# Memory tiles asked for on GpSimd's queue, and cumulated decays read back by pairs of heads, in a hybrid decoder layer

## The chip, the core and the metric

The kernel runs on one core of a Trainium2 chip. The core has five engines that work through instruction queues of their own: TensorE (PE in the profile) multiplies matrices, VectorE (DVE) and ScalarE (ACT) do elementwise work, GpSimd (POOL) does some elementwise work and issues DMAs, and SyncE (SP) only issues DMAs. ScalarE issues some DMAs too. Every queue is worked off in order: an instruction that waits holds up all that stand behind it. The metric is the device time of one execution in microseconds (us), less is better.

## What is computed

The reference is one layer: a SwiGLU feed-forward block, a mixer with two head groups (a Mamba-2 scan, here SSD, and differential attention), cross-attention into a memory of 256 tokens, and a second SwiGLU block. There are 512 tokens of width 1024, all in float32. Two pieces of it are touched here. The first is the decay matrix of the SSD scan, for each of 16 heads and 4 chunks of 128 tokens:

```python
la_cum = jnp.cumsum(la, axis=2)
seg = la_cum[:, :, :, None] - la_cum[:, :, None, :]
decay = jnp.exp(jnp.where(causal[None, None, :, :, None, None], seg, -jnp.inf))
y_diag = jnp.einsum('bclsg,bclsgr,bcsgrp->bclgrp', cb, decay, xdt)
```

The second is the normed memory, which cross-attention projects into keys and values:

```python
k = (mem_n @ w_ck).reshape(bsz, mlen, CROSS_HEADS, CROSS_HEAD_DIM)
v = (mem_n @ w_cv).reshape(bsz, mlen, CROSS_HEADS, CROSS_HEAD_DIM)
```

## The kernel before

Activations lie transposed, with features on the 128 partitions and tokens along the free dimension. Every float32 matrix product is done as three products of a reduced type: `split_into` (L152) makes from a tile a high part on ScalarE (`wh`, `hm`, `ysh`; L155, or L159 where a scale is applied) and the rest on VectorE (`wl`, `hm` low, `ysl`; L156, L160), and `mm3` multiplies high by high, high by low and low by high. One weight tile of 128x1024 therefore costs a load on SP's queue (`load_w`, L172, issue on L174), one split on ScalarE, one on VectorE and then 24 matmuls of 512 columns (`proj`). The raw weights have six buffers and the split ones three, so a load waits for the split of the load six before it.

The program is made in Python by a small planner, `Order` (L57). It steps through dense generators (the projections, in a fixed list) and adds the time of each matmul to a clock; chains (norms, heads, the SSD groups) are spawned with a due time and step in between when the clock has passed it. What the generators issue on SP's and on GpSimd's queues stays in the order of issue. The order on ScalarE and VectorE is chosen by the framework's scheduler from the same program.

Around the change:

- `steps` (L606) computes the cumulated decays `cum` as 128 tokens x 4 chunks x 16 heads. It transposes the 64 columns on TensorE (`pct`), copies them to SBUF (`ct_sb`) and stores them in DRAM as `cum_d`, 64 rows of 128, with row number 16 x chunk + head.
- `decays(g, j)` (L829) reads them back for two heads of group `g`, broadcast over the partitions, into one of two buffers (`gate` for j = 0, `th` for j = 1). It is called once for group 0 at the end of `steps` and then inside `group`, after the products that used the buffer.
- `group(g, ...)` (L838) is the chain of one SSD group of four heads. For each pair of heads ScalarE takes the exponential of the rows (L899), eight Relu of 128x128 (L901) and two exponentials (L902), VectorE masks with `cbm` (L903), and TensorE then does `pf` and `py`.
- `group_dense(g)` (L813) is the dense work of a group: four projections `xbc_tile` (products `pxbc`, then a convolution, L805 and L808, and a silu, L796 and L797) and two projections `pz`.
- `memory_prep` (L966) asks for the eight memory tiles (128x256 each) and then splits one at each step of its chain. It runs twice: in the first feed-forward block for the keys, and from `group_dense(3)` for the values, whose products `pcv` stand behind the last attention output.
- `block_sums_in_dram` (L1148) is a chain that makes sums of weight blocks for the second feed-forward block, off the way: SP loads a block into DRAM tiles `isum` and `wsum` (L1161), and some steps later GpSimd adds another to it with an accumulating DMA (L1165).

Besides its data, a DMA waits for its completion counter. SP's and ScalarE's DMAs together take eight counters in turn, GpSimd's take eight of their own, and a DMA that takes a counter waits until the DMA that had it before has landed. In the program before, the last four of the second eight memory loads on SP take the counters of the four decay reads that ScalarE issued for group 2, so each waits for one of those to land.

Of the kernel before, what the change touches and what calls it, by code (L numbers as in the profile page):

```python
# [17 lines left out]
P = 128  # L18
T = 512
D = 1024  # L20
KT = D // P
# [27 lines left out]
C_FFN1, C_MIX, C_CROSS, C_MEM, C_FFN2, C_SSD = (8 * i for i in range(6))  # L49
# [51 lines left out]
def body(tc, a, dbg=None):  # L101
    nc = tc.nc
# [12 lines left out]
    def nm(s):  # L115
        uid[0] += 1
        return f"{s}_{uid[0]}"

    def s2(s, dt=F32, shape=(P, T)):
        if math.prod(shape[1:]) <= T // 2:  # L120
            return sp.tile(list(shape), dt, tag="s1", name=nm(s), bufs=NHALF)
        return sp.tile(list(shape), dt, tag="s2", name=nm(s))

    def s4(s):
        return sp.tile([P, 4, T // 2], F32, tag=s, name=nm(s), bufs=1)

    def small(s, n, bufs=None):
        return tiny.tile([P, n], F32, tag=s, name=nm(s), bufs=bufs)

    def acc(s, shape=(P, T)):  # L130
        return acc_p.tile(list(shape), F32, tag="acc", name=nm(s))

    def aux(s, shape=(P, T)):
        return aux_p.tile(list(shape), F32, tag="aux", name=nm(s))

    def dump(name, t):
        if dbg and name in dbg:
            nc.sync.dma_start(dbg[name], t.bitcast(F32) if t.dtype == R32 else t)

    last, start, last_sum, recent, newest, newest_mm = [], [], [], [], [], []  # L140
    V, S, G = nc.vector, nc.scalar, nc.gpsimd
    od = Order()

    def mm(out, w, x, start, stop):
        od.t += (1 if w.dtype == R32 else 4) * (x.free_size() + 8) / 2400
        newest_mm[:] = [nc.tensor.matmul(out, w, x, start=start, stop=stop).ins]  # L146

    def transpose(out, x):
        od.t += 2 * (P + 8) / 2400
        nc.tensor.transpose(out, x, ident)  # L150

    def split_into(hi, lo, src, scale=None):  # L152
        if scale is None:
            return (
                S.activation(hi, src, AF.Copy),  # L155
                V.tensor_tensor(lo, src, hi.bitcast(F32), ALU.subtract),  # L156
            )
        return (
            S.activation(hi, src, AF.Copy, scale=scale),  # L159
            V.scalar_tensor_tensor(lo, src, scale, hi.bitcast(F32), ALU.mult, ALU.subtract),  # L160
        )

    def split(s, src, scale=None, half=False, n=T):
        if half:
            both = s2(s, R32, (P, 2, T // 2))
            hi, lo = both[:, 0], both[:, 1]
        else:
            hi, lo = s2(s + "h", R32, (P, n)), s2(s + "l", R32, (P, n))
        last[:] = [i.ins for i in split_into(hi, lo, src, scale)]
        return hi, lo  # L170
# [12 lines left out]
    @contextmanager  # L183
    def behind(ins):
        with ExitStack() as after:
            for i in ins:
                after.enter_context(tc.issue_after(i))
            yield
# [129 lines left out]
    def proj(ps, w, xs, ks=None):  # L318
        n = len(xs)
        for k in ks or range(n):  # L320
            mm3(ps, w, xs[k], k == 0, k == n - 1, wc=slice(k * P, (k + 1) * P))
            yield


    par = cp.tile([P, NPAR], F32, name="par")
# [195 lines left out]
    st_mix, h = Stat(), []  # L521
# [59 lines left out]
    def bc_c(t):  # L581
        return t[:, None, :].to_broadcast([P, 4, 16])

    def flat(t):
        return t.rearrange("p a b -> p (a b)")

    def col64(s):
        return cp.tile([P, 4, 16], F32, name=s)

    cum, cdec, dend, dth = col64("cum"), col64("cdec"), col64("dend"), col64("dth")  # L590
    cum_d = dram.tile([64, P], F32, name="cum_d")
# [14 lines left out]
    def steps(pdt):  # L606
        dtf = s2("dtf", shape=(32, T))
        S.activation(dtf, pdt, AF.Copy)
        ii = s2("ii", shape=(32, 16))
        nc.gpsimd.dma_start(ii, a["ii"])  # L610
        hb = s2("hb", shape=(P, 2, 16))
        nc.gpsimd.dma_start(hb, a["hb"].partition_broadcast(P))
        yield 4.5
        pdk = aux("pdk", (P, 4, 16))
        for c in range(4):
            mm(pdk[:, c, :], dtf[:, c * P : (c + 1) * P], ii, True, True)
        dtr, dta, dtz, dte, dtp, la = (s2("dt", shape=(P, 4, 16)) for _ in range(6))
        V.tensor_tensor(dtr, pdk, bc_c(hb[:, 0]), ALU.add)

        S.activation(dta, dtr, AF.Abs)  # L620
        S.activation(dte, dta, AF.Exp, scale=-1.0)
        V.tensor_scalar(dtz, dte, 2.0, None, ALU.add)
        V.reciprocal(dtz, dtz)
        V.tensor_tensor(dtz, dtz, dte, ALU.mult)
        V.tensor_tensor(dte, dtz, dtz, ALU.mult)
        V.tensor_scalar(dtp, dte, 1.0 / 19, None, ALU.mult)
        for n in range(17, 2, -2):
            V.scalar_tensor_tensor(dtp, dtp, 1.0 / n, dte, ALU.add, ALU.mult)
        V.scalar_tensor_tensor(dtp, dtp, 1.0, dtz, ALU.add, ALU.mult)
        V.tensor_scalar(dtr, dtr, 0.0, None, ALU.max)  # L630
        V.scalar_tensor_tensor(dtr, dtp, 2.0, dtr, ALU.mult, ALU.add)
        dump("dt", dtr)
        ea = small("ea", 16, bufs=1)
        G.tensor_tensor(ea, euler[:, 0:1].to_broadcast([P, 16]), hb[:, 1], ALU.pow)
        V.scalar_tensor_tensor(la, dtr, -1.0, bc_c(ea), ALU.mult, ALU.mult)
        V.tensor_scalar(dth, dtr, 0.5, None, ALU.mult)
        yield 7.5
        pcum = aux("pcum", (P, 2, 64))
        mm(pcum[:, 0], tri, flat(la), True, True)
        mm(pcum[:, 1], ones, flat(la), True, True)  # L640
        V.tensor_copy(flat(cum), pcum[:, 0])
        V.tensor_tensor(flat(dend), pcum[:, 1], flat(cum), ALU.subtract)
        S.activation(flat(cdec), pcum[:, 1], AF.Exp)
        S.activation(dend, dend, AF.Exp)
        V.tensor_scalar(dend, dend, 0.5, None, ALU.mult)
        yield 1.5
        pct = aux("pct", (64, P))
        transpose(pct, flat(cum))
        ct_sb = s2("ct_sb", shape=(64, P))
        V.tensor_copy(ct_sb, pct)  # L650
        nc.gpsimd.dma_start(cum_d, ct_sb)
        for j in range(2):
            decays(0, j)
        dump("cum", cum)
# [138 lines left out]
    def silu2(src):  # L793

        th = s2("th2")
        S.activation(th, src, AF.Tanh, scale=0.5)  # L796
        V.scalar_tensor_tensor(th, th, 1.0, src, ALU.add, ALU.mult)  # L797
        return th

    def xbc_tile(n, dst):  # L800
        ps = acc("pxbc")
        yield from proj(ps, load_w(a["wxbc"][n]), h)
        y = s2("conv")
        cw = C_CONVW + 4 * n
        S.activation(y, ps, AF.Identity, bias=par[:, C_CONVB + n : C_CONVB + n + 1], scale=par[:, cw + 3 : cw + 4])  # L805
        for j in (2, 1, 0):
            d = 3 - j
            V.scalar_tensor_tensor(y[:, d:], ps[:, : T - d], par[:, cw + j : cw + j + 1], y[:, d:], ALU.mult, ALU.add)  # L808
        dst.append(silu2(y))
# [3 lines left out]
    def group_dense(g):  # L813
        bc, xs, zs = [], [], []
        if g == 3:
            od.spawn(memory_prep(hm2, 3.0), 1.0)
        yield from xbc_tile(8 + g, bc)
        yield from xbc_tile(12 + g, bc)
        for j in range(2):
            yield from xbc_tile(2 * g + j, xs)  # L820
        od.spawn(group(g, bc[0], bc[1], xs, zs), W["g0"])
        for j in range(2):
            ps = acc("pz")
            yield from proj(ps, load_w(a["wz"][2 * g + j]), h)
            zs.append(silu2(ps))

    rows_of = {}

    def decays(g, j):  # L829

        rows_of[g, j], both = [], s4(("gate", "th")[j])
        for hh in range(2):
            r = both[:, 2 * hh : 2 * hh + 2].rearrange("p a (b c) -> p (a b) c", c=P)
            hd = 4 * g + 2 * j + hh
            S.dma_start(r, bass.AP(cum_d.tensor, cum_d.offset + hd * P, [[0, P], [16 * P, 4], [1, P]]))
            rows_of[g, j].append(r)

    def group(g, bt, ct, xs, zs):  # L838
        hsl = slice(4 * g, 4 * g + 4)
# [51 lines left out]
        for j in range(2):  # L891
# [21 lines left out]
            if g < 3:  # L913
                decays(g + 1, j)
# [34 lines left out]
    st_mem = Stat(MEM)  # L949
    ck, cv = [], []  # L950

    def memory_tile(k):
        mk = s2("mem", shape=(P, MEM))
        nc.sync.dma_start(mk, a["memT"][k])
        return mk

    def memory_norm():
# [5 lines left out]
        yield 3.0  # L963
        yield from st_mem.finish(42.0)

    def memory_prep(dst, apart=2.0):  # L966
        mem = [memory_tile(k) for k in range(KT)]
        for k, mk in enumerate(mem):
            with behind(recent):
                dst.append(split("hm", mk, par[:, C_MEM + k : C_MEM + k + 1], True))  # L970
            yield apart

    def memory_keys():
# [67 lines left out]
    hm, hm2 = [], []  # L1041
# [368 lines left out]
```

## Time and profile before

| What | us |
|---|---|
| Runs, median of 3 (lowest to highest) | 1328.93 (1327.06 to 1331.06) |
| The profiled execution | 1330.36 |
| Its span, first to last instruction | 1328.6 |
| TensorE busy in it | 1307.6 |
| VectorE, ScalarE, GpSimd busy in it | 946.4, 667.5, 114.1 |

The profile is of one execution. Times in a timeline are counted from the first instruction. A row of the timeline gives the start, the duration, the engine, the line of the kernel, the operation, output and inputs by the program's names, the shape, how many instructions were merged, and in brackets how long the engine had been idle before it and what ended that. The rows with a `q` behind the engine (SPq, ACTq, POOLq) are DMA issues. A row that merges several issues spans the time from the first to the last, waits included. "PEclk" is the granted clock of TensorE as a share of the full one.

### The profile page before, as it was taken

What the parts mean: (1) busy time and instruction counts of PE and PEld (TensorE: products, weight loads), DVE (VectorE), ACT (ScalarE), POOL (GpSimd) and SP (SyncE); (2) the same over time, 40 slices, a digit from 0 to 9 for tenths busy, and PEclk for the clock granted to TensorE, in tenths of its full rate; (3) what the DMA queues carried; (4) which work ended last, traced back from release to release, by engine and by line L of the source; (5) the groups of instructions that cost most, each with busy time, mean ns of one, the idle gap of its engine ahead of it and who ended that gap; (6) DMA issues with size and microseconds to landing.
All of it is one profiled execution on the core that took longest, in us unless ns stands there. A gap on an engine that the chain in (4) does not pass through costs nothing.

```text
span 1328.6 us, 19969 instructions
## 1 busy us (share of the span) xinstructions
PE 1307.6 (98%) x7767; PEld 1137.1 (86%) x7767; DVE 946.4 (71%) x1498; ACT 667.5 (50%) x1116; POOL 114.1 (9%) x127
## 2 busy tenths in 40 slices
PE   9999999999999999999999999999999999999997
PEld 7898998899887778777888777888889999989995
DVE  6874778477786586557867677645688877877886
ACT  6442445154454565346545456434455645554564
POOL 0000010000020111100012021120001100000001
PEclk9999999999999999999999899999999999999999
DMA  7444577555583734673365757675138976666662
GB/s 271 112 126 127 125 203 246 132 146 172 189 251 89 212 73 105 185 241 88 88 186 128 192 138 221 196 192 165 62 114 227 250 228 176 191 195 179 188 201 94
DMA packets 74143, 222.71 MB, mean 168 GB/s; under 512 B 8424, under 2 KB 20176, under 8 KB 73696
## 3 DMA queue, kind: packets, MB, share of 16 engines
q1 hardware_dynamic: 52400, 174.42, 39.1%
q0 software_dynamic: 11904, 40.45, 16.8%
q10 hardware_dynamic: 9744, 6.56, 2.4%
q8 instruction: 61, 1.00, 0.3%
q14 instruction: 34, 0.28, 0.1%
HBM read 219.24 MB, written 50.91 MB: 203 GB/s over the span
## 4 chain that ended last, share of the span: by engine, by line
PE 93%; DVE 3%; ACT 2%; issue 1%; POOL 1%; DMA 0%; POOLq 0%; SPq 0%; ACTq 0%; DVEq 0%
PE qb L240 12%; PE po L146 10%; PE pm L146 9%; PE qe L240 8%; PE qa L240 8%; PE pxbc L146 7%; PE pk L146 3%; PE pq L146 3%; PE pcq L146 3%; PE pv L146 3%; PE pz L146 3%; PE ob L1195 3%; PE oa L1195 2%; PE oe L1195 2%; PE pa L146 2%; PE pg L146 2%
## 5 line engine op out<-in xcount | busy, mean ns | idle before, releaser
L155 ACT ACTIVATE wh<-wr 128x1024 fp32r<-128x1024 f32 (+2 forms) x311 | 316.7, 1021 | 391.9 <-issue 60.8
L156 DVE TENSOR_TENSOR wl<-wr,wh 128x1024 fp32r<-128x1024 f32 (+2 forms) x311 | 366.0, 1179 | 133.0 <-ACT wh L155 126.1
L146 PE MATMUL po<-gl,wh 128*128 128x512 f32 x176 | 68.5, 390 | 0.0
L146 PE MATMUL po<-gh,wh 128*128 128x512 f32 x176 | 68.4, 391 | 0.0
L146 PE MATMUL po<-gh,wl 128*128 128x512 f32 x176 | 68.4, 389 | 0.0
L240 PE MATMUL qa<-hml,wh 128*128 128x256 f32 x216 | 61.1, 283 | 0.0
L240 PE MATMUL qa<-hmh,wl 128*128 128x256 f32 x216 | 61.1, 283 | 0.0
L240 PE MATMUL qa<-hmh,wh 128*128 128x256 f32 x216 | 61.1, 283 | 0.0
L146 PE MATMUL pxbc<-hnh,wh 128*128 128x512 f32 x128 | 53.3, 416 | 1.8 <-ACT wh L155 1.8
L146 PE MATMUL pxbc<-hnh,wl 128*128 128x512 f32 x128 | 51.5, 402 | 0.8 <-DVE wl L156 0.8
L146 PE MATMUL pxbc<-hnl,wh 128*128 128x512 f32 x128 | 51.3, 401 | 0.0
L709 ACT ACTIVATE ec<-ec,mn 128x512 f32<-128x512 f32 (+3 forms) x64 | 35.4, 555 | 23.8 <-DVE mn L708 23.8
L507 DVE TENSOR_TENSOR upd<-po,row 128x512 f32<-128x512 f32 x24 | 16.6, 690 | 39.4 <-PE po L146 39.2
L240 PE MATMUL qe<-s31h,wl 128*128 128x256 f32 x152 | 43.2, 284 | 0.5 <-DVE wl L156 0.5
L240 PE MATMUL qb<-s24h,wl 128*128 128x256 f32 x152 | 43.1, 284 | 0.5 <-DVE wl L156 0.5
L240 PE MATMUL qe<-s31h,wh 128*128 128x256 f32 x152 | 43.1, 284 | 0.0
L240 PE MATMUL qe<-s24h,wh 128*128 128x256 f32 x152 | 43.0, 283 | 0.0
L240 PE MATMUL qb<-s31h,wl 128*128 128x256 f32 x152 | 43.0, 283 | 0.0
L240 PE MATMUL qb<-hmh,wh 128*128 128x256 f32 x152 | 43.0, 283 | 0.0
L240 PE MATMUL qb<-hml,wh 128*128 128x256 f32 x152 | 43.0, 283 | 0.0
L240 PE MATMUL qb<-hmh,wl 128*128 128x256 f32 x152 | 43.0, 283 | 0.0
L240 PE MATMUL qe<-s24h,wl 128*128 128x256 f32 x152 | 43.0, 283 | 0.0
(444 smaller groups left out, 4036.8 us busy)
## 6 DMA issues: line engine op xcount, KB each, us to landing
wr<-in_f2q SPq DMA_DIRECT2D x44, 512.0 KB, 4.4
wr<-in_f1q SPq DMA_DIRECT2D x40, 512.0 KB, 4.4
isum<-in_f2q SPq DMA_DIRECT2D x22, 512.0 KB, 6.0
wr<-isum SPq DMA_DIRECT2D x22, 512.0 KB, 4.3
wsum<-in_f2b SPq DMA_DIRECT2D x20, 512.0 KB, 8.4
wr<-wsum SPq DMA_DIRECT2D x20, 512.0 KB, 4.6
wr<-in_f1q POOLq DMA_DIRECT2D x16, 512.0 KB, 5.6
wr<-in_f1o SPq DMA_DIRECT2D x16, 512.0 KB, 3.8
```

Source lines behind the costliest of these rows:

```text
L146: newest_mm[:] = [nc.tensor.matmul(out, w, x, start=start, stop=stop).ins]
L155: S.activation(hi, src, AF.Copy),
L156: V.tensor_tensor(lo, src, hi.bitcast(F32), ALU.subtract),
L240: newest_mm[:] = [nc.tensor.matmul(out, a_[:, wc], b_, start=first and f == 0 and kp == 0 and j == 0, stop=kp == n - 1 and j == 2, skip_gr ...
L507: V.tensor_tensor(upd, po, row4, ALU.mult)
L709: S.activation(ec[:, :n], ec[:, :n], AF.Exp, bias=mn, scale=-1.0, accum_out=sm[c][:, i : i + 1])
L1195: newest_mm[:] = [nc.tensor.matmul(ps, a_[:, ts], b_[:, ws], start=first and k == 0 and j == 0, stop=k == n - 1 and j == 2, skip_group_che ...
```

## The change

There are two edits. The memory tiles of the second `memory_prep` are asked for on GpSimd's queue: four ahead, and then one more at each step. The first `memory_prep` and `memory_norm` keep SP's queue and ask for all eight at once. The cumulated decays are copied into an order by head before the transpose, so that `cum_d` has row number 4 x head + chunk; a pair of heads is then eight rows in a row, 4 KB, and is read by one DMA of 128x1024 in place of two DMAs of 128x4x128.

```diff
@@ steps
         yield 1.5
+        by_hd = s2("by_hd", shape=(P, 16, 4))
+        V.tensor_copy(by_hd.rearrange("p h c -> p c h"), cum)
         pct = aux("pct", (64, P))
-        transpose(pct, flat(cum))
+        transpose(pct, flat(by_hd))
@@ group_dense
         if g == 3:
-            od.spawn(memory_prep(hm2, 3.0), 1.0)
+            od.spawn(memory_prep(hm2, 3.0, 4, nc.gpsimd), 1.0)
@@ decays
-        rows_of[g, j], both = [], s4(("gate", "th")[j])
-        for hh in range(2):
-            r = both[:, 2 * hh : 2 * hh + 2].rearrange("p a (b c) -> p (a b) c", c=P)
-            hd = 4 * g + 2 * j + hh
-            S.dma_start(r, bass.AP(cum_d.tensor, cum_d.offset + hd * P, [[0, P], [16 * P, 4], [1, P]]))
-            rows_of[g, j].append(r)
+        both = s4(("gate", "th")[j]).rearrange("p a (b c) -> p (a b) c", c=P)
+        S.dma_start(both, bass.AP(cum_d.tensor, cum_d.offset + (4 * g + 2 * j) * 4 * P, [[0, P], [1, 8 * P]]))
+        rows_of[g, j] = [both[:, 4 * hh : 4 * hh + 4] for hh in range(2)]
@@ memory_tile, memory_prep
-    def memory_tile(k):
+    def memory_tile(k, queue=nc.sync):
         mk = s2("mem", shape=(P, MEM))
-        nc.sync.dma_start(mk, a["memT"][k])
+        queue.dma_start(mk, a["memT"][k])
         return mk
-    def memory_prep(dst, apart=2.0):
-        mem = [memory_tile(k) for k in range(KT)]
-        for k, mk in enumerate(mem):
+    def memory_prep(dst, apart=2.0, ahead=KT, queue=nc.sync):
+        mem = [memory_tile(k, queue) for k in range(ahead)]
+        for k in range(KT):
+            if k + ahead < KT:
+                mem.append(memory_tile(k + ahead, queue))
             with behind(recent):
-                dst.append(split("hm", mk, par[:, C_MEM + k : C_MEM + k + 1], True))
+                dst.append(split("hm", mem[k], par[:, C_MEM + k : C_MEM + k + 1], True))
             yield apart
```

The built programs show what this moves. TensorE's order is the same instruction for instruction. SP's queue loses the eight loads, which stood between a load of `in_wxbc` and one of `in_f2b`. GpSimd's queue gets them behind the second `ndiag` of group 1 and the `isum` accumulation that follows it, ahead of the two `wsum` accumulations there and partly between them (six, one `wsum`, two, the other `wsum`). ScalarE's queue has eight DMA issues fewer. VectorE has one copy more. ScalarE's and VectorE's orders differ otherwise in one place, which belongs to the time from 727 to 762 us of the profile before: of the splits of the weights loaded there, the first two move forward on both engines (on ScalarE the first to ahead of the two `ysh`, the second to right behind `btk`), and the third and fourth by a few places.

## The prediction

> **What bounds the kernel now.** I read the page first: engine shares, then the chain that ended last.
>
> ```profile
> span 1328.6 us, 19969 instructions
> ...
> PE 1307.6 (98%) x7767; PEld 1137.1 (86%) x7767; DVE 946.4 (71%) x1498; ACT 667.5 (50%) x1116; POOL 114.1 (9%) x127
> ...
> PE 93%; DVE 3%; ACT 2%; issue 1%; POOL 1%; DMA 0%; POOLq 0%; SPq 0%; ACTq 0%; DVEq 0%
> ```
>
> TensorE is the bound; it lacks only 1328.6 - 1307.6 = 21.0 us, and its matmuls are the same in both programs. An edit to queues can only change the gaps between them, or their pace. So the next view is what TensorE waited for (total, times, longest).
>
> ```profile
> PE init L342 <- ACT ones_r L340: 2.4, 1, 2.4
> PE pxbc L146 <- ACT wh L155: 1.8, 1, 1.8
> ...
> PE pxbc L146 <- DVE wl L156: 0.8, 1, 0.8
> ```
>
> The two `pxbc` waits belong together. The timeline of TensorE and two stretches of the view by windows (length, PE, PEld, DVE, ACT, POOL busy, granted clock, DMA share, GB/s) show where.
>
> ```profile
> 742.64 0.39 PE L146 MATMUL pxbc<-hnh,wl 128*128 128x512 f32 x1
> ...
> 744.84 0.51 PE L146 MATMUL pxbc<-hnh,wh 128*128 128x512 f32 x1 [1.81 <-ACT wh L155]
> ...
> 746.59 0.79 PE L146 MATMUL pxbc<-hnh,wl 128*128 128x512 f32 x1 [0.82 <-DVE wl L156]
> ...
> 751.88 0.47 PE L146 MATMUL pxbc<-hnh,wl 128*128 128x512 f32 x1
> 752.19 0.40 PE L146 MATMUL pxbc<-hnh,wh 128*128 128x512 f32 x1
> 752.42 0.40 PE L146 MATMUL pxbc<-hnl,wh 128*128 128x512 f32 x1
> 740.00:746.00 6.00, 3.96 (x16) 2.48 (x14) 5.03 (x9) 5.72 (x12) 0.00 (x0) 0.93 1.01 292
> 746.00:752.00 6.00, 5.41 (x13) 4.25 (x14) 4.93 (x7) 2.38 (x4) 0.00 (x0) 0.50 0.49 151
> ```
>
> Undisturbed starts are 0.23 us apart (752.19 to 752.42); the 13 from 746.59 to 752.19 are 5.60 / 13 = 0.43 apart, at a granted clock of 0.50. From 742.64 to 752.19 there are 16 starts, by count 16 x 0.23 = 3.68 us, but 9.55 passed: **5.9 us lost**. Of them 13 slow steps from 746.59 take 5.60 - 2.99 = 2.6, the two gaps the other 3.3.
>
> Why was the split late? ScalarE and VectorE:
>
> ```profile
> 729.19 1.29 ACT L155 ACTIVATE ysh<-y 128x512 fp32r<-128x512 f32 x2 [1.59 <-DVE y L944]
> ...
> 735.56 0.49 ACT L869 ACTIVATE btk<-pbt 128x384 f32<-128x384 f32 x1 [4.59 <-PE pbt L150]
> ...
> 736.81 0.50 ACT L159 ACTIVATE hm<-mem,par 128x256 fp32r<-128x256 f32 x1
> 737.21 1.27 ACT L899 ACTIVATE e<-gate 64x512 f32<-64x512 f32 x2
> ...
> 743.74 1.99 ACT L155 ACTIVATE wh<-wr 128x1024 fp32r<-128x1024 f32 x2
> 743.09 0.69 DVE L903 TENSOR_TENSOR gate<-gate,cbm 128x512 f32<-128x512 f32 x1
> 745.33 1.21 DVE L156 TENSOR_TENSOR wl<-wr,wh 128x1024 fp32r<-128x1024 f32 x1
> ```
>
> The two splits (743.74) stand in ScalarE's queue behind the decay work of group 2 (737.21 on), though ScalarE idled 4.59 us before 735.56. Their weights came on SP's queue:
>
> ```profile
> 692.26 0.33 SPq L174 DMA_DIRECT2D wr<-in_wxbc  x1
> 692.63 29.07 SPq L954 DMA_DIRECT2D mem<-in_memT  x8
> ...
> 722.34 1.01 SPq L174 DMA_DIRECT2D wr<-in_wxbc  x2
> SPq L954 <- DMA th<-cum_d: 12.4, 2, 6.5
> SPq L954 <- DMA gate<-cum_d: 10.9, 2, 7.7
> ```
>
> The eight memory loads hold SP for 29.07 us, 23.3 of it waiting for decay reads to land. The next weights are asked for at 722.34.
>
> **The change part by part.** *SP without the loads: -5.9 us.* The load behind 692.26 then waits for a raw buffer, freed by the split six loads earlier:
>
> ```profile
> 692.64 1.06 ACT L155 ACTIVATE wh<-wr 128x1024 fp32r<-128x1024 f32 x1 [1.66 <-PE pm L146]
> 696.60 0.98 ACTq L835 DMA_DIRECT2D gate<-cum_d  x2
> 701.82 1.04 ACT L155 ACTIVATE wh<-wr 128x1024 fp32r<-128x1024 f32 x1
> 706.80 0.93 ACTq L835 DMA_DIRECT2D th<-cum_d  x2
> wr<-in_wxbc SPq DMA_DIRECT2D x16, 512.0 KB, 7.2
> ```
>
> With some 2.5 us for both halves of a split the two loads go at about 695 and 704 and land, at 7.2, by 712. In the changed program their splits stand ahead of `ysh` (729.19) and behind `btk` (done at 735.56 + 0.49 = 736.05), so the data are there and both are done by about 731 and 739, VectorE's 1.21 included. TensorE needs them at 742.64 + 0.23 = 742.87 and one tile (24 x 0.23 = 5.5) later: both gaps go, and with them, as I take it, the slow stretch. The splits fall into ScalarE's 4.59 us of idle time and, for the second, push what follows by 1.05. Next late could be the third split, which was behind 743.74 too: TensorE now needs it at 742.87 + 11 + 1.8 for `pf` and `py`, about 755, and its place is now near 744.
>
> The Trainium skill, page DMA: Bandwidth & Descriptors, section "Issuing engines are not separate DMA queues", says that issuing from several engines saves only sequencer time, since all use the same 16 DMA engines. By it this edit would be worth eight issues off the path, so nothing; the row of 29.07 us for eight loads speaks of waits, not of issue time, and I go by the row. The rule's result is the second rival below.
>
> *The loads on GpSimd: 0.* In the changed program they stand behind these two:
>
> ```profile
> 722.96 1.48 POOL L368 TENSOR_TENSOR ndiag<-ident,cl 128x512 fp32r<-128x512 f32 x1
> 724.39 0.88 POOL L1165 DMA_DIRECT2D isum<-isum  x1
> ...
> 783.08 1.28 POOL L931 TENSOR_TENSOR ysq<-ysq,ysq 128x512 f32<-128x512 f32 x1 [56.10 <-ACT ysq L929]
> ```
>
> So the first goes at about 725.3, not at 692.63, and ScalarE wants its tile at about 737.9 (736.81 + 1.05). Eight issues near 0.9 each, and the later ones' waits for earlier DMAs of that queue, are hidden: GpSimd's next work is at 783.08. What a plain 128 KB load takes on this queue, between accumulations, no row shows; the nearest are:
>
> ```profile
> mem<-in_memT SPq DMA_DIRECT2D x24, 128.0 KB, 6.3
> ii<-in_ii POOLq DMA_DIRECT2D x1, 2.0 KB, 8.8
> wsum<-in_f2b POOLq DMA_DIRECT2D x2, 512.0 KB, 17.7
> rel_z<-rel_d POOLq DMA_DIRECT2D x1, 2560.0 KB, 27.4
> 757.04 1.09 PE L146 MATMUL py<-gate,xdt 128*64 128x128 f32 x16
> ```
>
> (The `wsum` row is of 724.9 to 727.5 us, the two accumulations behind which the loads would else stand.) From below 6.3, from above 17.7; I take 8.8, a plain load on the same queue: landed at 734.1, in time. At 17.7 it lands at 743.0, and ScalarE waits 5.1 us at its first `hm`. That still costs nothing: the decay product behind it ends at 743.78 (743.09 + 0.69), 744.8 with the moved split, and `py` wants it at 757.04 - 5.9 = 751.1, a cover of 6.3. What is queued behind that `hm` is all of group 2's decay work and the later splits.
>
> *Decays by pairs: 0.* Eight reads in place of 16 save ScalarE half of 0.98 each time, 4 us over the run, where it idles. A pair now takes between the 7.2 us of the weight loads of its size above and the 14.9 that pass from 706.80 until SP's last memory load, which waits for such reads, has gone (692.63 + 29.07 = 721.70). Issued at 696.60 and used at 737.21, either is hidden.
>
> *The copy to `by_hd`: 0.*
>
> ```profile
> L641 DVE COPY cum<-pcum x1: 216/216/216, 416.4 to 416.4; 128x64 f32<-128x64 f32 x1
> ```
>
> The same size costs 0.22 us; strided, at most the double, 0.4. It sits ahead of the `cum_d` store, whose rows group 2 uses at 737.21, some 320 us later.
>
> **Sum.** 1328.6 - 5.9 = 1322.7 us of span. The profiled execution was 1330.36, 1.8 outside the span and 1.4 above the median of 1328.93; the median moves by the same 5.9: **1323.0 us**.
>
> **The rivals.** (1) *The slow stretch stays.* It may not come from the gaps, or another one follows a gap elsewhere, once the time of everything behind 742 has moved. Then only 3.3 come off: 1325.7. For it: no other wait in this run has a slow stretch behind it to compare. Against: it begins inside the gap. The Trainium skill, page TensorE: Matmul & The Clock Gate, section "HAM oscillation — how this bites in real kernels", wants gaps above some 3.4 us before the clock halves; the gaps here are 1.81 and 0.82, so by that rule the stretch isn't theirs, and this rival's time follows; the trace has 0.50 right behind them, so I doubt it here.
>
> (2) *Hidden anyway.* The gap is ScalarE's backlog, and SP's freedom changes nothing: 1328.9. Against it: in the built program the two splits have moved ahead of that backlog.
>
> (3) *Slower: the first memory tile is late on GpSimd's queue.* It decides from a landing 12.6 + 6.3 = 18.9 us after 725.3. At 27.4, the longest landing on that queue, the tile is there at 752.7, TensorE waits 8.5 us for `py` and gets a slow stretch of 2.6: 1328.9 - 5.9 + 11.1 = 1334.1. For it: accumulations of 17.7 us ahead and behind. Against: that row is of 512 KB, four times the bytes.
>
> **How the numbers follow.** Forecast 0.66, rival 1 0.10, rival 2 0.09, rival 3 0.15: the forecast asks that all three steps (SP, splits, memory tile) go in time. What this kernel's runs can tell from no change is about 0.3%, 4.0 us, so below 1324.9. With the runs' own spread of 2 us to either side, faster gets 0.60 of the forecast's share and 0.02 of rival 1's, 0.62; slower all of rival 3 and 0.03 of rival 2, 0.18; the same the rest, 0.20. Range: 1320.5 (forecast less that spread and a little for shorter DMAs) to 1329.5 (through rivals 1 and 2, short of rival 3).
>
> **What would show it.** After: no `pxbc` wait on `wh` near 742 and no window at 0.50 there; SP asks for the two `in_wxbc` loads near 695 and 704; the first `hm` of the second set starts near 738 without a wait on a DMA; `cum_d` reads are 512 KB and land in under 14.9 us. I am wrong if TensorE still stops between 740 and 760, if it stops at `py` for `gate`, or if a new half-clock stretch stands elsewhere.

## The result, and the profile after

| | before | after |
|---|---|---|
| Median of 7 runs (lowest to highest), us | 1328.89 (1327.06 to 1331.06) | 1324.69 (1324.03 to 1326.74) |
| Ratio to before, with its 95% interval | | 0.9972 (0.996 to 0.9983) |
| Profiled execution, and its span, us | 1330.36, 1328.6 | 1324.87, 1323.1 |
| TensorE busy in it, us | 1307.6 | 1304.0 |

The changed kernel is 4.2 us faster by the medians, and 5.5 us by the two profiled executions. The forecast was 1323.0, within 1320.5 to 1329.5. The difference between 4.2 and 5.5 is the most instructive part of this case.

First the view of TensorE's waits in the profile after (total, times, longest). Lines of the changed kernel's code stand one or two off those before (the decay reads on L834, the memory loads on L953).

```profile
PE init L342 <- ACT ones_r L340: 2.4, 1, 2.4
PE nrow L146 <- POOL ndiag L368: 1.1, 1, 1.1
PE nrow L146 <- DVE ndiag L368: 0.9, 2, 0.5
PE pm L146 <- DVE x L788: 0.9, 1, 0.9
PE pn L146 <- POOL ysq L930: 0.8, 2, 0.5
```

Both `pxbc` rows are gone, and nothing new of their size stands in their place. Two stretches of the windows view (length, PE, PEld, DVE, ACT, POOL busy, granted clock, DMA share, GB/s) show the same place:

```profile
740.00:746.00 6.00, 6.00 (x28) 4.97 (x27) 4.55 (x9) 5.17 (x11) 0.00 (x0) 1.00 0.10 35
746.00:752.00 6.00, 6.00 (x42) 4.97 (x40) 5.08 (x9) 3.17 (x5) 0.00 (x0) 1.00 0.52 178
```

Before, TensorE was busy for 3.96 and 5.41 us of these twelve, and the clock was 0.93 and 0.50; now it has no gap and the full clock. The timelines of SP, ScalarE, VectorE, GpSimd and TensorE after show the chain behind it:

```profile
694.86 8.86 SPq L174 DMA_DIRECT2D wr<-in_wxbc  x2
...
727.83 1.06 ACT L155 ACTIVATE wh<-wr 128x1024 fp32r<-128x1024 f32 x1 [0.34 <-PE pz L146]
...
735.90 1.06 ACT L155 ACTIVATE wh<-wr 128x1024 fp32r<-128x1024 f32 x1
...
737.35 0.50 ACT L159 ACTIVATE hm<-mem,par 128x256 fp32r<-128x256 f32 x1
...
744.17 1.05 ACT L155 ACTIVATE wh<-wr 128x1024 fp32r<-128x1024 f32 x1
729.61 1.22 DVE L156 TENSOR_TENSOR wl<-wr,wh 128x1024 fp32r<-128x1024 f32 x1
...
737.00 1.22 DVE L156 TENSOR_TENSOR wl<-wr,wh 128x1024 fp32r<-128x1024 f32 x1 [1.08 <-DMA wr<-in_woa]
...
745.75 1.22 DVE L156 TENSOR_TENSOR wl<-wr,wh 128x1024 fp32r<-128x1024 f32 x1
724.89 3.55 POOL L953 DMA_DIRECT2D mem<-in_memT  x6
750.22 0.83 PE L146 MATMUL pf<-th,st 128*128 128x128 f32 x6
750.98 1.09 PE L146 MATMUL py<-gate,xdt 128*64 128x128 f32 x16
752.01 0.50 PE L146 MATMUL pxbc<-hnh,wh 128*128 128x512 f32 x1
...
755.56 0.39 PE L146 MATMUL pxbc<-hnh,wh 128*128 128x512 f32 x1
```

SP asks for the two weights at 694.86 and again when 8.86 us are over, ScalarE splits them at 727.83 and 735.90 instead of at 743.74, and the first `hm` starts at 737.35 with no wait for a DMA. `py` starts at 750.98 instead of 757.04. TensorE was already 0.12 us earlier ahead of this place (`btk` at 735.44 against 735.56), so 5.9 us come off here; it keeps them to its last matmul, which ends 5.9 us earlier.

### The profile page after: what moved, and what is told of

It is laid out like the page before. It is cut to its first block, busy times and chain, and to the rows that moved or that the text cites. A ratio compares the mean times of both kernels' runs of the same rounds, so it can differ in the third digit from the quotient of the medians.

```text
span 1323.1 us, 19981 instructions
## 1 busy us (share of the span) xinstructions
PE 1304.0 (99%) x7767; PEld 1134.4 (86%) x7767; DVE 945.9 (71%) x1499; ACT 669.4 (51%) x1116; POOL 117.9 (9%) x135
## 4 chain that ended last, share of the span: by engine, by line
PE 89%; issue 4%; DVE 3%; ACT 1%; DMA 1%; POOL 1%; SPq 0%; POOLq 0%; DVEq 0%; ACTq 0%
PE qb L240 12%; PE po L146 10%; PE pm L146 9%; PE qe L240 8%; PE qa L240 8%; PE pxbc L146 5%; PE pk L146 3%; PE pq L146 3%; PE pcq L146 3%; PE pv L146 3%; PE ob L1196 3%; PE pz L146 2%; PE oa L1196 2%; PE oe L1196 2%; PE pg L146 2%
```

## The experiments

**The kernel before, once more.** The profiled execution of before holds a stretch at half clock. Does every execution?

> The kernel before, unchanged. The changed kernel's median fell by 4.2 us, the two profiled executions differ by 5.5. Theory: the two waits at `pxbc` stand in every execution (1.8 and 0.8 us), but the half-clock stretch behind them comes in some executions only, at 2.6 us a time; then the mean granted clock differs among the runs, 0.995 with the stretch and 0.997 or 0.998 without it, and the runs at 0.995 are some 2.6 us longer. Rival: the stretch always follows, every run has 0.995, and the spread of 4 us has another cause.

The new profile has both waits and no stretch. Its windows at the same place, then a grid of 3.41 us laid through it:

```profile
740.00:746.00 6.00, 3.44 (x14) 2.21 (x13) 5.04 (x8) 5.41 (x11) 0.00 (x0) 1.00 0.84 275
746.00:752.00 6.00, 5.72 (x25) 4.72 (x26) 4.62 (x7) 2.92 (x5) 0.00 (x0) 1.00 0.36 116
...
740.87:744.29 3.42, 1.84 (x9) 1.17 (x7) 2.76 (x5) 3.41 (x8) 0.00 (x0) 1.00 1.01 334
744.29:747.70 3.41, 2.15 (x8) 1.48 (x9) 3.38 (x5) 1.85 (x4) 0.00 (x0) 1.00 0.36 136
```

Its waits are 1.81 and 1.02 us, its time 1327.56. The 28 runs of the kernel before that went with this group of experiments fall into three groups by their mean granted clock over the whole run:

| Mean granted clock | Runs of 28 | Median, us |
|---|---|---|
| 0.998 | 10 | 1327.86 |
| 0.996 or 0.997 | 9 | 1329.15 |
| 0.995 | 9 | 1330.61 |

I read the groups as no stretch, one of 3.41 us or one of 6.83 us. The profile of before is in the last group and has 6.83 us; this one has 0.998 and none; for the middle there is a profile with the same two waits, that of the decays by pairs below (0.996, 3.41 us). The theory holds, with 2.75 us between the ends (1330.61 - 1327.86) where 2.6 was expected and a step in the middle that was not. Of this experiment's own eleven runs nine fit and two do not: 1331.39 at 0.996 and 1330.82 at 0.997 are 2.2 and 1.7 us above the middle group's median, and neither was profiled. Its ratio to the other runs of the same kernel is 1.0002 (0.9993 to 1.0011).

**Only the queue of the memory tiles.** The changed kernel without the edit of the decays:

```diff
-        by_hd = s2("by_hd", shape=(P, 16, 4))
-        V.tensor_copy(by_hd.rearrange("p h c -> p c h"), cum)
...
-        transpose(pct, flat(by_hd))
+        transpose(pct, flat(cum))
...
-        S.dma_start(both, bass.AP(cum_d.tensor, cum_d.offset + (4 * g + 2 * j) * 4 * P, [[0, P], [1, 8 * P]]))
...
+            S.dma_start(r, bass.AP(cum_d.tensor, cum_d.offset + hd * P, [[0, P], [16 * P, 4], [1, P]]))
...
```

> Memory tiles on GpSimd's queue, four ahead; decays stored and read as before (16 reads of 256 KB). Theory: SP's queue without the eight loads is the whole gain: 1324.7 us, no wait of `pxbc` near 742, no stretch at half clock, ScalarE's two splits near 728 and 736. Rival (the slow decay reads cost as well): between 1326 and 1329, with a wait at `pxbc` or `py` that is left.

1324.76 us, ratio 0.9969 (0.9957 to 0.9981); no wait of `pxbc`, no stretch. The queue of the memory tiles is the whole gain. The profiled execution is 2.1 us above this median (1326.89) and lost that time at the start of the program, far ahead of the edited work: its first `pa` products are 0.43 us apart until 11.53, while in the changed kernel's profile they are 0.23 us apart from 6.75 on. Its last matmul ends 2.0 us later (1315.17 against 1313.14). Why the start differs was not tested.

**Only the decays by pairs.** The changed kernel with the memory tiles on SP, eight ahead:

```diff
-            od.spawn(memory_prep(hm2, 3.0, 4, nc.gpsimd), 1.0)
+            od.spawn(memory_prep(hm2, 3.0, 8, nc.sync), 1.0)
```

> Decays stored by head and read by pairs; memory tiles on SP, eight ahead, as before. The order of ScalarE's work is that of the kernel before. Theory A (ScalarE's order sets the wait, not the moment at which the weights land): SP is held for 10 to 15 us in place of 29, the weights land well before 740, yet the two splits still start near 743.7 and TensorE waits 1.8 and 0.8 us as before: 1328.9. Theory B (the late weights set it): the waits fall with the hold, 1324.7 to 1326.

1329.07 us, ratio 0.9998 (0.9989 to 1.0007). SP's, ScalarE's and TensorE's timelines, and a window:

```profile
692.35 17.90 SPq L953 DMA_DIRECT2D mem<-in_memT  x8
...
710.89 1.01 SPq L174 DMA_DIRECT2D wr<-in_wxbc  x2
743.39 1.99 ACT L155 ACTIVATE wh<-wr 128x1024 fp32r<-128x1024 f32 x2
744.49 0.50 PE L146 MATMUL pxbc<-hnh,wh 128*128 128x512 f32 x1 [1.81 <-ACT wh L155]
743.77:747.18 3.41, 1.67 (x6) 1.10 (x7) 3.37 (x5) 1.85 (x3) 0.00 (x0) 1.00 0.00 0
747.18:750.59 3.41, 3.41 (x10) 2.65 (x9) 3.40 (x5) 2.14 (x4) 0.00 (x0) 0.50 0.47 154
```

The quick reads shorten the hold of SP's queue from 29.07 to 17.90 us, and the weights are asked for 11.4 us earlier (710.89 against 722.34). The splits start at 743.39 all the same, the wait is the same 1.81 us. Theory A holds: when the weights land does not decide it.

**Four ahead on SP, decays as before.** The kernel before with the four-ahead form of `memory_prep`:

```diff
-            od.spawn(memory_prep(hm2, 3.0), 1.0)
+            od.spawn(memory_prep(hm2, 3.0, 4, nc.sync), 1.0)
```

> Decays as before; memory tiles on SP, four ahead and one more at each step. In the built program four of them stand where all eight did and the others two or one between the next loads; ScalarE's order is that of before but for one exponential. Theory A: the splits stay behind group 2's decay work, both waits at `pxbc` stay: 1328 to 1330. Theory B (fewer loads ahead are enough): 1324.7 to 1326.

1329.58 us, ratio 1.0003 (0.9995 to 1.0012), with waits of 2.33 and 1.02 us at `pxbc`: the splits stay behind the decay work, and the wait stays.

**The two splits put back behind the decay work.** The changed kernel, with one order forced:

```diff
+                if g == 2 and j == 0 and hh == 1:
+                    hold[:] = [ex.ins]
...
+            for i in hold:
+                after.enter_context(tc.issue_after(i))
             recent[:] = [i.ins for i in split_into(hi, lo, raw)]
```

(`ex` is the exponential of L901; `hold` is emptied behind `py`.)

> The changed kernel, with one thing forced: ScalarE may issue the two splits only behind the second exponential of group 2's first pair of heads, where they stood before. SP's and GpSimd's queues are those of the changed kernel. Theory A (the place in ScalarE's queue makes the wait): weights asked for at 695 and 704 as in the changed kernel, and yet both waits at `pxbc` are back, some 1.8 and 1.0 us, the splits start near 743.7, and the time is 1327.3 to 1331, median near 1329. Theory B (SP's freedom makes the gain): 1324.7.

1329.39 us, ratio 1.0001 (0.9992 to 1.001). Its SP, ScalarE and TensorE:

```profile
695.01 8.85 SPq L175 DMA_DIRECT2D wr<-in_wxbc  x2
744.29 1.99 ACT L156 ACTIVATE wh<-wr 128x1024 fp32r<-128x1024 f32 x2
745.39 0.50 PE L147 MATMUL pxbc<-hnh,wh 128*128 128x512 f32 x1 [2.33 <-ACT wh L156]
...
746.34 0.50 PE L147 MATMUL pxbc<-hnh,wh 128*128 128x512 f32 x1 [0.22 <-ACT wh L156]
```

SP runs as freely as in the changed kernel, the second weight is asked for 40 us before its split, and all of the gain is gone. The place of the two splits in ScalarE's queue is the cause. The second wait differs in form from the one expected (0.22 on `wh`, not 1.0 on `wl`), and TensorE's order differs there too: one product that needs `wl` stands later (at 753.61). In the two experiments on one edit each TensorE's order is that of the kernel before, and there too the gain goes with the place of the splits.

**Eight ahead on GpSimd.**

```diff
-            od.spawn(memory_prep(hm2, 3.0, 4, nc.gpsimd), 1.0)
+            od.spawn(memory_prep(hm2, 3.0, 8, nc.gpsimd), 1.0)
```

> The changed kernel with all eight memory tiles asked for at once on GpSimd's queue, instead of four ahead and one at each step. In the built program the loads stand ahead of both accumulations; SP's queue is the same, ScalarE's but for one exponential. Theory: the number ahead is worth nothing, 1324.7 us. Rival (the accumulations between the loads keep the order or the buffers): 1326 to 1330.

1324.98 us, ratio 0.9968 (0.9956 to 0.9981): the number ahead is worth nothing.

**The first memory tile late: three loads, five loads.**

```diff
-        queue.dma_start(mk, a["memT"][k])
+        for _ in range(times):
+            queue.dma_start(mk, a["memT"][k])
```

(`times` is 3 or 5 for the first of the second set, 1 otherwise.)

> The changed kernel with the first memory tile loaded three times in a row into its buffer, each load behind the landing of the one before: at 6.3 us each it lands near 745 in place of 731. ScalarE's first product of the second set then waits, and group 2's decay work behind it. By the cover of the third rival (the first `hm` may start up to 6.6 us late before `py` waits): `py` waits 0 to 2 us, 1324.7 to 1327. If the cover is larger (the scheduler has also moved the third split ahead): 1324.7 and no wait. If it is smaller: 1327 to 1332.

> The same with five loads: the tile lands near 757. The scheduler sees the lateness and has moved `py` back by some matmuls and the weights' splits forward. By the cover the decay product ends near 764.5, and `py` waits for it 10 us or more: 1333 to 1338. If the moved order hides it: 1324.7 to 1328.

With three: 1324.45 us, ratio 0.9967 (0.9955 to 0.998). With five: 1332.05 us, 1.0024 (1.0015 to 1.0033). The tile lands earlier than expected in both. GpSimd's, ScalarE's and TensorE's timelines with three loads:

```profile
724.31 0.89 POOL L954 DMA_DIRECT2D mem<-in_memT  x1
729.41 0.56 POOL L954 DMA_DIRECT2D mem<-in_memT  x1 [4.21 <-DMA mem<-in_memT]
732.76 3.17 POOL L954 DMA_DIRECT2D mem<-in_memT  x6 [2.78 <-DMA mem<-in_memT]
742.19 1.06 ACT L155 ACTIVATE wh<-wr 128x1024 fp32r<-128x1024 f32 x1 [3.75 <-PE pxbc L146]
743.16 0.49 ACT L159 ACTIVATE hm<-mem,par 128x256 fp32r<-128x256 f32 x1
750.41 1.09 PE L146 MATMUL py<-gate,xdt 128*64 128x128 f32 x16
```

A load behind the landing of another goes every 5.1 or 3.4 us, not 6.3. The scheduler has put the third split ahead of the first `hm`, and that split holds it until 743.16. So `hm` is 5.8 us later than in the changed kernel, by that split and not by its tile, and `py` still does not wait: the cover of 6.3 us is borne out from below. With five loads `hm` starts at 744.11 and the order has moved more: `py` stands further back among the `pxbc` matmuls. Its TensorE waits, and a grid of 3.41 us:

```profile
PE pn L146 <- POOL ysq L930: 3.9, 2, 2.9
...
779.37:782.78 3.41, 1.78 (x9) 1.24 (x9) 3.09 (x3) 2.18 (x4) 2.21 (x2) 1.00 0.42 120
782.78:786.19 3.41, 3.41 (x15) 3.01 (x15) 2.17 (x5) 0.00 (x0) 1.36 (x2) 0.50 0.89 201
```

It pays not at `py`, as expected, but later: 3.9 us at `pn`, and two stretches of 6.83 us at half clock (from 782.78 and from 823.74). How much of its 7.4 us over the changed kernel each part takes was not separated, and which amount of lateness alone decides was not tried with the order held.

**The chain of the memory tiles spawned later.** If the order on ScalarE decides, the loads can stay on SP. Four forms: on the changed kernel with SP, eight ahead (`mem_later`) and with GpSimd, four ahead (`later_pool`), and on the kernel before, 12 us (`later_only`) and 20 us (`later20`). The last is this edit alone:

```diff
-            od.spawn(memory_prep(hm2, 3.0), 1.0)
+            od.spawn(memory_prep(hm2, 3.0), 20.0)
```

> Decays by pairs; memory tiles on SP again, eight at once, but their chain is spawned 12 us later, so that on SP they stand behind two more weight loads; in the built program the two splits stand where the changed kernel has them. Theory A: SP is held by the loads for 10 us or more and it costs nothing, no wait at `pxbc` near 742, 1324.7 as the changed kernel (1324 to 1326). Rival (loads on SP cost by themselves, whatever the order): 1327 to 1330 with a wait for a later weight.

> The kernel before with one number changed: the second chain of the memory tiles is spawned 12 us later instead of 1. Memory tiles on SP, eight at once, decays in 16 reads as before. Theory A (what counts is what stands ahead of what in ScalarE's queue): as with pairs of heads, 1321.1 us, no wait at `pxbc`. Rival: with the slow decay reads SP is held until 725 or so behind the two weight loads, and a later weight is late: 1323 to 1327 with a wait of `pxbc` or `pz`.

> The changed kernel with the chain spawned 12 us later, its loads on GpSimd's queue, four ahead. Theory A: the queue does not matter once the order does, 1321.1 us (1320.5 to 1321.8). Rival: the loads on GpSimd cost by themselves (behind an accumulation, landing later): 1322 to 1325, or gain something: under 1320.

> The kernel before with the chain spawned 20 us later. Further off group 2's work of ScalarE, but nearer to the products that use the tiles. If the gain of the later chain came from ScalarE being free for group 2's second pair of heads: 1321 again, or up to 1 us less. If the tiles now come too late for `pcv`: 1323 to 1330, with a wait of `pcv` for `hm`.

| Chain spawned | Queue, decays | Median, us | Ratio to before (95%) |
|---|---|---|---|
| 12 us later | SP, by pairs | 1321.08 | 0.994 (0.9928 to 0.9953) |
| 12 us later | SP, as before | 1323.29 | 0.9955 (0.9942 to 0.9967) |
| 12 us later | GpSimd, by pairs | 1322.02 | 0.9951 (0.9938 to 0.9965) |
| 20 us later | SP, as before | 1320.26 | 0.9932 (0.9919 to 0.9944) |

All four beat the kernel before, and the last also beats the changed kernel by 4.4 us. None has a wait at `pxbc` on `wh` near 742. Three of the four expectations were missed: `mem_later` came out some 3 us below its range; `later_only` came out in its rival's range, but without the wait at `pxbc` or `pz` that the rival named; and `later_pool` lies just outside the range of its theory, at the lower edge of its rival's. SP's and TensorE's rows of the last:

```profile
708.61 17.29 SPq L954 DMA_DIRECT2D mem<-in_memT  x8
761.08 1.09 PE L146 MATMUL py<-th,xdt 128*64 128x128 f32 x16
```

In the changed kernel the second pair of heads comes later, and what hangs on it waits:

```profile
766.93 0.43 PE L146 MATMUL py<-th,xdt 128*64 128x128 f32 x2 [0.29 <-DVE th L902]
769.13 1.09 PE L146 MATMUL py<-th,xdt 128*64 128x128 f32 x14
```

The loads hold SP for 17.29 us even there and it costs nothing. `py` of the second pair starts 5.9 us earlier, and the waits at `pm` (0.9), `pn` (0.8), `py` (0.3) and most of `nrow`'s on GpSimd (1.1, now 0.3) are gone. These waits are 2.8 of the 4.3 us between the two spans (1323.1 and 1318.8). Where the rest comes from is not shown. These four programs also differ from the changed kernel in TensorE's own order, from about 761 us on: the sixteen `py` above stand in one block and ahead of products that precede them in the changed kernel, where they come in two blocks. So the further gain is not that of ScalarE's order alone, and the parts were not separated. With 12 us and the old reads, 2.2 us of it are missing: there the quick reads are of use, or the slightly different order that the scheduler makes with them; the two were not separated.

## Why the prediction came out as it did

**The direction and the place: right.** TensorE lost 5.9 us between 742.64 and 752.19, and in the two profiled executions that is what came off: 5.9 us at TensorE, 5.5 in the span.

**The sum: its last step failed.** "The median moves by the same 5.9" took the profiled execution's loss for that of a typical one. The two gaps (3.3) stand in both profiles of before; the half-clock stretch (2.6), by the granted clock of the runs, has its full length in 9 of 28 only, half of it in 9, and none in 10. Against the runs without a stretch the gain is 1327.86 - 1324.69 = 3.2 us, the gaps' 3.3; over all runs it is 4.2. The forecast was 1.7 us too low for that. The profile had a hint: that execution was 1.4 us above the median, and the three times shown spread over 4 us.

**"SP without the loads": right in its place, wrong in its reason.** The prediction saw that the splits stood behind the decay work and that they had moved, but it took the row of 29.07 us as the cause: weights late, hence splits late. The times forecast for the loads (695 and 704; measured 694.86 and 703.7) and for the ends of the splits (731 and 739; 730.83 and 738.22) were met. But weights that land early bring nothing while the splits stand behind the decay work (pairs only, 1329.07), a free SP queue brings nothing either (order forced, 1329.39), and a held one costs nothing there once the splits stand ahead of that work (17.29 us, 1320.26). The edit works because the scheduler, given another SP queue, writes ScalarE's work in another order. Why it does so was not tested beyond the built programs.

**The third split** was done at 746.97 (745.75 + 1.22) and needed at 755.56, where the third weight tile's products begin; about 755 was forecast. It was in time, as forecast.

**The loads on GpSimd: 0, right.** The tile was taken to land in 8.8 us; the median here is 6.3, as on SP in the kernel before. In the kernel with only the queue changed it is 9.6, and the time is the same. The rows of the changed kernel, with those of the decay reads:

```profile
mem<-in_memT POOLq DMA_DIRECT2D x8, 128.0 KB, 6.3
gate<-cum_d ACTq DMA_DIRECT2D x4, 512.0 KB, 4.4
th<-cum_d ACTq DMA_DIRECT2D x4, 512.0 KB, 6.2
```

**The decays by pairs: 0, right in time, wrong in size.** A pair was put between 7.2 and 14.9 us; it takes 4.4 or 6.2, where half a pair took 10.1 or 15.5 before (issues grouped over the whole run).

**The copy to `by_hd`: right.** 0.22 us, strided or not:

```profile
L648 DVE COPY by_hd<-cum x1: 216/216/216, 416.7 to 416.7; 128x64 f32<-128x64 f32 x1
```

**Rival 1** (the stretch stays, 1325.7) was wrong for the changed kernel, which has none in its profile and 0.997 or 0.998 in all seven runs, but its doubt was the right one: the stretch's 2.6 us could not be counted in full. **Rival 2** (hidden anyway): its premise, that the loss is ScalarE's backlog and not SP, was right; its conclusion was not, since the edit moves that backlog's order. **Rival 3** (the tile late on GpSimd's queue) did not come; with three loads the first `hm` started 5.8 us later and it cost nothing. With five it started 6.8 us later (744.11) and the time rose by 7.4, by another wait than the one named; but TensorE's order had moved as well, so the lateness alone is not priced.

**The clock rule.** The clock fell to 0.50 behind a gap of 1.81 us (before), and behind one of 1.81 and one of 1.02 (pairs only). The Trainium skill, page TensorE: Matmul & The Clock Gate, section "HAM oscillation — how this bites in real kernels", gives idle gaps above some 3.4 us as the rule; the traces here don't bear that out as a condition, since no gap shown here is that long.

## What to carry to other kernels

A DMA queue that stands still is not yet a cause: ask which instruction waited last, and whether it would start earlier if its data were there; here it was the split's place in ScalarE's queue. So compare the built orders of all engines before pricing a queue edit, and look for a smaller edit that changes them: one spawn time, which moves the orders of SP, ScalarE and TensorE together, gave twice the gain of the change (8.7 against 4.2 us). And before a loss of one profiled execution is put into a sum, see where that execution stands among the runs: a stretch at half clock may have its full length in a third of them only.

## What the runs showed of the hardware

In these traces the granted clock changes on a grid of 3.41 us that is not tied to the program: every stretch at half clock within the work is 3.41 or 6.83 us long, and in the two profiles of the kernel before the steps begin at different times (741.77 and 740.87). Whether a stretch follows went by how long TensorE was busy in one step of the grid. Busy for 1.61 us (before), 1.67 (pairs only), 1.55 (four ahead on SP), 1.75 (order forced), 1.42 or 1.78 (five loads) of 3.41, the next step ran at half clock; busy for 1.84 us (the kernel before once more) or 1.93 (four ahead on SP) it did not. The row of before, to set beside the pairs above:

```profile
741.77:745.19 3.42, 1.61 (x8) 1.01 (x6) 2.72 (x5) 3.41 (x7) 0.00 (x0) 1.00 1.08 326
745.19:748.60 3.41, 2.59 (x7) 1.62 (x6) 3.41 (x5) 1.85 (x4) 0.00 (x0) 0.50 0.59 196
748.60:752.01 3.41, 3.41 (x10) 2.64 (x9) 2.33 (x4) 1.07 (x2) 0.00 (x0) 0.50 0.43 117
```

Here a gap of 0.82 us lies in the first half-clock step and a second such step follows; where the first was busy throughout (747.18 in pairs only) the clock came back after one. That is no rule: with five loads the step from 782.78 was busy throughout, and the next one, 786.19 to 789.61, still ran at 0.50. What ends a stretch stays open. So two short waits close together can cost more than their length, by chance of the grid. Inside the work the bound lies between 1.78 and 1.84 us busy in these few traces, near half of a step. One step at the end of TensorE's work does not fit: in `later_pool` it was busy for 1.66 us (1308.39 to 1311.80), and the next one kept the full clock. For the execution without a stretch the grid was carried back from the clock's fall at the end of the run.
